# The first MLP matrix's weight sums: built in DRAM scratch by copies and accumulating transfers, or grown in their own SBUF tiles between uses

## The chip, the cores and the metric

The kernel runs on one core of a Trainium2 chip. TensorE multiplies matrices, VectorE, ScalarE and GpSimd (POOL) work elementwise, and transfers are issued on the queues of SyncE (SP), ScalarE (ACT) and POOL and carried out by 16 DMA engines that the queues share. The metric is the device time of one execution in microseconds.

## The reference

Two layers on x of 512 tokens by 1024 features, float32. Each layer has a mixer (a projection of the normalised x into attention, an mLSTM memory and gates, two branch projections, an output projection) and an MLP. The change is in the MLP's weights:

```python
    x = x + mixed @ w_out

    u = jax.nn.relu(rmsnorm(x, norm_ffn) @ w_ff1)
    return x + (u * u) @ w_ff2
```

w_ff1 is 1024 x 4096 and w_ff2 is 4096 x 1024 for each layer.

## The kernel before

**Split products.** Every float32 operand is split into a rounded high part and the rest (ScalarE makes the high part, VectorE subtracts, lines 916 and 917 for the MLP's weights), and a product is three matmuls (`mm3`, line 211). TensorE's work is therefore in matmuls, and ScalarE and VectorE have a split to make for each weight block.

**Seven products instead of eight.** In the MLP, blocks of two by two are multiplied with seven products instead of eight, which needs sums of weight blocks. With b11, b12, b21, b22 the four quarters (row half, column half), the sums are A = b11 + b12, D = b12 + b22, B = b11 + D and C = b21 + B (`SUMS`, line 373). Of the seven products, numbers 1, 2 and 3 use plain quarters (b11, b21, b22) and 5, 6, 7 and 4 use A, B, D and C. The left operands are sums of the other matrix's quarters, made once (`left_blocks`, line 1056, for the first matrix; `left`, line 1013, for the second).

**Parts.** The MLP's width of 4096 is done in four parts of 1024 columns (two times 512). `first(part, i, u)` (line 1096) makes half a part of relu(h @ W1)^2 with seven slots of 24 matmuls 128x256, its accumulators in two PSUM banks of one pair and in two auxiliary banks. `second(part, u)` (line 966) multiplies a part by W2 with seven slots of two runs of 12 matmuls 128x512. Part 0 of the first matrix is done with plain products (`Plain`, line 1153), since its left operand is not ready in time for the sums.

**Order of the work.** Lines 1196 to 1208 write the order out: each slot of `second` is followed by 2, 2, 2, 2, 3, 3 and 0 slots of the next part's two `first` blocks. A unit is one run. `go` (line 1217) prepares the weights of the unit five ahead (`SPL`), that is, it emits its load and its split, and then the unit's matmuls. Five buffers of split weights (`spl`) make a split wait until the matmuls five units back are done. Raw tiles of the first matrix rotate over three buffers (`raws`), loaded on SP's queue by `load1` (line 946); at the head of the MLP the first seven loads are queued behind marked loads of the mixer's output projection (`w_marks`, line 905). Raw tiles of the second matrix (`raw2`) have a buffer of their own by name and half, and many of W2's sums are made in them by VectorE (`plus`, line 924).

**Sums in DRAM.** The sums of W1 for parts 1 to 3, and some of W2 (D of every part, all four of the last part), are built in DRAM scratch (`Sums`, line 385), in halves of 512 KB. Each half of a sum is first copied from the weights (or from another sum) by a transfer on ScalarE's queue, and then a transfer on POOL's queue adds the other addend to it. So that these jobs are spread, each is tied to a split: the copy is queued behind the last split on ScalarE, and the addition behind a marker (line 404), a tiny POOL copy that reads the last split's result. `plan_sums` (line 414) lists the jobs, and `beat` (line 426) does the next one: 32 beats lie in the mixer (line 866), four at the head of the MLP (line 1188), and then one at every second unit (line 1227). A layer has 79 jobs, three of them empty.

Of the kernel before, what the change touches and what calls it, by code (L numbers as in the profile page):

```python
# [8 lines left out]
F32 = mybir.dt.float32  # L9
# [4 lines left out]
ALU = mybir.AluOpType  # L14
# [21 lines left out]
def hybrid_kernel(ctx, tc, x, norm_mix, w_in, att_q_norm, att_k_norm, att_sinks, m_gate_bias,  # L36
# [157 lines left out]
        return wh, wl  # L194

    last_wh = [None, None]
    w_loads, w_marks, by_turns = [], [], []
    last_split = [None, None]

    def split(src, scale=None, get=lambda: slot(F32R)):  # L200
# [66 lines left out]
    def rsqrt(dst, v, tag):  # L267

        shape = list(v.shape)
        t = sm(shape, tag + "t")  # L270
        sc.activation(t, v, AF.Ln)
        sc.activation(dst, t, AF.Exp, scale=-0.5)
        t2 = sm(shape, tag + "u")
# [100 lines left out]
    mark = const.tile([1, 2], F32, name="mark")  # L374
    jobs, sums = [], {}

    def w1_rows(l, part, k, n, h):
        r0, c0 = T * k + 2 * P * h, DFF // 2 * n + T * part
        return w_ff1[l, r0:r0 + 2 * P, c0:c0 + T]
# [5 lines left out]
    class Sums:  # L385
# [11 lines left out]
            return self.to(b, h) if b in SUMS else self.rows(*b, h)  # L397

        def copy(self, n, h):
            with tc.issue_after((last_split if by_turns else last_wh)[0].ins):  # L400
                nc.scalar.dma_start(self.to(n, h), self.of(SUMS[n][0], h))

        def add(self, n, h):
# [9 lines left out]

    def plan_sums(l):

        s = [None] + [Sums(l, part, w1_rows) for part in range(1, 4)]
        p = [Sums(l, part, w2_rows, "D") for part in range(3)] + [Sums(l, 3, w2_rows)]
        sums.clear()
        sums.update({(1, part): s[part] for part in range(1, 4)})
        sums.update({(2, part): p[part] for part in range(4)})  # L420
        jobs.extend(s[1].copies("DABC") + s[1].adds("DAB") + p[0].copies("D") + s[1].adds("C")
                    + s[2].copies("DABC") + p[0].adds("D") + s[2].adds("DAB") + p[1].copies("D") + s[2].adds("C")
                    + s[3].copies("DABC") + p[1].adds("D") + s[3].adds("DAB") + p[2].copies("D") + s[3].adds("C")
                    + p[3].copies("DABC") + p[2].adds("D") + p[3].adds("DAB") + [lambda: None] * 3 + p[3].adds("C"))

    def beat():
        if jobs:
# [2 lines left out]
    def beats(*at):  # L430
        return [(a, beat) for a in at]

    def mixer(l, norm, late, order, phase):
# [134 lines left out]
        def rope(xv, b, nh):  # L568

            r0 = 0 if nh == HQ else 8  # L570
            ct, st = tabs[nh != HQ]
            ve.tensor_tensor(xv, xv, rqk[:, b, r0:r0 + nh].unsqueeze(2).to_broadcast([P, nh, HD]), op=ALU.mult)
            t1 = sm([P, nh, ROPE], f"rp{nh}")
            t2 = sm([P, nh, ROPE], f"rq{nh}")
# [317 lines left out]
    def mlp(l, norm, late, phase):  # L892
# [62 lines left out]
        def gain(t, j, ps, sign, done=False):  # L955

# [9 lines left out]
        def second(part, u):  # L966
# [15 lines left out]
            def weights(which, h):  # L982
                if end:
                    tag = "pqpqpqp"[(1, 5, 6, 3, 7, 2, 4).index(which)]
                    plain = {1: (0, 0), 3: (1, 1), 2: (1, 0)}.get(which)
                    load(b11, tag, h, block(*plain, h) if plain else
                         sums[2, 3].to({5: "A", 6: "B", 7: "D", 4: "C"}[which], h))
                    return w_split(b11[h])
                if which == 1:
                    load(b11, "p", h, block(0, 0, h))  # L990
                    load(b12, "q", h, block(0, 1, h))
                    r = w_split(b11[h])
                    plus(b11[h], b11[h], b12[h])
                elif which == 5:
                    load(b22, "q", h, block(1, 1, h))
                    r = w_split(b11[h])
                    plus(b11[h], b11[h], b22[h])
                elif which == 6:
                    r = w_split(b11[h])
                elif which == 3:  # L1000
                    r = w_split(b22[h])
                elif which == 7:
                    load(b12, "q", h, sums[2, part].to("D", h))
# [92 lines left out]
        def first(part, i, u):  # L1096

            c0 = T * part + H * i
            ps = {}

            def weights(which):
                at = {1: (0, 0), 3: (1, 1), 2: (1, 0)}.get(which)
                if at:
                    k, n = at
                    return load1(w_ff1[l, T * k:T * (k + 1), DFF // 2 * n + c0:DFF // 2 * n + c0 + H])
                return load1(sums[1, part].t[{5: "A", 6: "B", 7: "D", 4: "C"}[which]][:, H * i:H * (i + 1)])

            def to(t, n):
                return u[i][:, 2 * n:2 * n + 2, H * t:H * (t + 1)]
# [13 lines left out]
            def slot(which, bank, fresh, *done):  # L1123

                ws = []

                def run():
                    if fresh:
                        if bank == "a":
                            two = banks("f")  # L1130
                            ps["a"], ps["b"] = two[:, 0, :], two[:, 1, :]
                        elif bank != "b":
# [12 lines left out]

                return Slot([lambda: ws.append(weights(which))], [run], end)

            return [slot(1, "a", True, (copy, 0, 0)), slot(5, "b", True, (copy, 1, 1)),
                    slot(2, "c", True, (finish, 0, 0)), slot(6, "a", False, (copy, 0, 1)),
                    slot(3, "b", False, (finish, 0, 1)), slot(7, "a", False, (finish, 1, 1), (copy, 1, 0)),  # L1150
                    slot(4, "d", True, (finish, 1, 0))]

        class Plain:


            def __init__(self, i, n, which):
                self.c0, self.i, self.n, self.which, self.w = DFF // 2 * n + H * i, i, n, which, {}

            def load(self, h):
                self.w[h] = load1(w_ff1[l, T * h:T * (h + 1), self.c0:self.c0 + H])  # L1160

            def step(self, k):
                if k == 0:
# [19 lines left out]
        for h in range(2):  # L1183
            for f in plain:
                f.load(h)
        by_turns.append(1)
        weave([(0.5, lambda k=k, f=f: f.step(k)) for k in range(KT) for f in plain],
              late + [(6.5, norm.inverse)] + beats(1.6, 2.1, 2.6, 3.1))
        by_turns.clear()
        for f in plain:  # L1190
            f.evac(us[0])
        us.append(new_u(1))
# [24 lines left out]
        def go(i, s, n):  # L1217
# [68 lines left out]
```

## Time and profile before

| | us |
|---|---|
| three runs | 1327.36, 1330.26, 1337.07 |
| median of the runs | 1330.26 |
| the profiled execution's own time | 1333.33 |
| its span, from the first to the last instruction | 1331.5 |
| TensorE busy | 1298.1 |
| VectorE busy | 954.5 |
| ScalarE busy | 768.5 |
| POOL busy | 215.3 |

PE is TensorE, DVE is VectorE, ACT is ScalarE, and a q behind a name is the queue on which it issues transfers. A group's line shows the line of the kernel, the engine, the operation, the tile written and the tile read, the shapes, how often, then the busy time and the mean in ns of one, then the idle time of the engine just ahead of them with what ended it. Tiles are named without their numbers: raw is a raw weight tile, wh and wl its split, sum a sum in DRAM scratch. In the chain of waits a line has a start, a duration and what it was; in a timeline the same, with the idle time ahead of it in brackets. In a table of stretches each engine has its busy time and the number of its instructions, and then come the granted clock, the share of the 16 DMA engines that was busy, and GB/s. In a list of queues q1 is SP's, q10 is ScalarE's and q0 is POOL's, each with packets, MB and their share of the 16 engines' time. In a list of transfers the last number is the median time from issue to landing.

The layers' MLPs lie at about 320 to 650 us and 980 to 1330 us, the mixers ahead of them.

### The profile page before, as it was taken

Reading aid. Unit: us, or ns where it says so; the run is one execution under the profiler, and the core shown is the slowest. Engines: PE = TensorE matmul, PEld = TensorE weight load, DVE = VectorE, ACT = ScalarE, POOL = GpSimd, SP = SyncE. Lnnn points to the kernel's source line nnn. Section 1 sums busy time; section 2 is a strip of 40 time slices with the busy share of each in tenths; the row PEclk is TensorE's granted clock in tenths of the full one; section 3 lists DMA queues with packets and bytes.
Section 4 is the critical chain, followed back from the end, with each engine's and each line's share of the span. In section 5 each row is a group of like instructions: output and inputs, shape, how many; then the busy total and the mean of one; then the engine's idle time right before and its main releaser. Section 6 shows DMA issues by size and latency. Waiting matters only on the chain.

```text
span 1331.5 us, 19392 instructions
## 1 busy us (share of the span) xinstructions
PE 1298.1 (97%) x6966; PEld 1103.2 (83%) x6966; DVE 954.5 (72%) x1493; ACT 768.5 (58%) x1367; POOL 215.3 (16%) x371
## 2 busy tenths in 40 slices
PE   8999999998999999999999999999999999999998
PEld 6877788887888989899778777888888899899986
DVE  4688764475568698887946887644766687979786
ACT  5468765553366556666545687654544565666663
POOL 4523310200000210020005233102000002102100
PEclk9999999999999999999999999999999999999999
DMA  5547455847356989897415465557382579997954
GB/s 151 172 137 148 120 153 150 180 120 216 100 135 230 252 200 285 238 243 223 154 29 181 136 140 127 151 155 170 119 260 71 152 249 242 233 309 198 270 160 142
DMA packets 154176, 236.36 MB, mean 178 GB/s; under 512 B 11608, under 2 KB 67008, under 8 KB 154080
## 3 DMA queue, kind: packets, MB, share of 16 engines
q1 hardware_dynamic: 111776, 154.76, 36.8%
q0 software_dynamic: 21056, 39.98, 18.2%
q10 hardware_dynamic: 21248, 40.38, 9.8%
q8 instruction: 55, 0.90, 0.3%
q14 instruction: 41, 0.34, 0.1%
HBM read 232.99 MB, written 81.79 MB: 236 GB/s over the span
## 4 chain that ended last, share of the span: by engine, by line
PE 78%; DVE 11%; DMA 4%; ACT 3%; issue 3%; POOL 0%; SPq 0%; ACTq 0%; DVEq 0%; POOLq 0%
PE mm L47 67%; PE aux L47 9%; DMA raw<-in_w_ff_dram 3%; PE aux L51 2%; DVE wl L917 2%; DVE wl L193 2%; DMA w<-in_w_in_dram 1%; ACT wh L916 1%; DVE ul L909 1%; DVE x L961 1%; ACT wh L192 0%; DVE s L931 0%; ACT t L658 0%; DVE a L724 0%; DVE t L645 0%
## 5 line engine op out<-in xcount | busy, mean ns | idle before, releaser
L47 PE MATMUL mm<-i,wh 128*128 128x512 f32 (+1 forms) x1280 | 354.4, 362 | 0.5 <-ACT t L842 0.5
L917 DVE TENSOR_TENSOR wl<-raw,wh 128x1024 fp32r<-128x1024 f32 x212 | 257.1, 1220 | 81.2 <-ACT wh L916 81.0
L916 ACT ACTIVATE wh<-raw 128x1024 fp32r<-128x1024 f32 x212 | 223.4, 1055 | 151.4 <-PE mm L47 113.5
L47 PEld LDWEIGHTS mm<-i,wh 128*128 128x128 f32 x1280 | 224.3, 189 | 32.9 <-ACT t L842 0.9
L47 PE MATMUL mm<-i,wl 128*128 128x512 f32 (+1 forms) x640 | 229.7, 359 | 0.0
L193 DVE TENSOR_TENSOR wl<-w,wh 128x512 fp32r<-128x512 f32 (+1 forms) x208 | 142.1, 684 | 110.6 <-ACT wh L192 107.0
L192 ACT ACTIVATE wh<-w 128x512 fp32r<-128x512 f32 (+1 forms) x208 | 126.9, 612 | 135.4 <-PE mm L47 96.6
L404 POOL COPY mark<-wh 1x2 f32<-1x2 f32 x76 | 47.7, 628 | 813.1 <-ACT wh L916 660.1
L47 PE MATMUL mm<-wh,ul 128*128 128x512 f32 x448 | 175.7, 392 | 2.6 <-DVE ul L909 2.1
L47 PE MATMUL mm<-wh,uh 128*128 128x512 f32 x448 | 175.7, 392 | 1.5 <-DVE x L961 1.5
L47 PE MATMUL mm<-wl,uh 128*128 128x512 f32 x448 | 175.2, 391 | 0.6 <-DVE wl L917 0.6
L47 PE MATMUL mm<-wh,i 128*128 128x512 f32 (+1 forms) x512 | 149.7, 370 | 0.4 <-ACT wh L192 0.4
L47 PEld LDWEIGHTS mm<-i,wl 128*128 128x128 f32 x640 | 120.9, 189 | 17.7
L47 PE MATMUL mm<-hs,wh 128*128 128x256 f32 x576 | 105.7, 284 | 0.0
L47 PEld LDWEIGHTS mm<-wh,i 128*128 128x128 f32 x512 | 92.3, 189 | 15.9 <-ACT wh L192 0.8
L47 PEld LDWEIGHTS mm<-wh,ul 128*128 128x128 f32 x448 | 84.4, 188 | 22.4 <-DVE ul L909 5.0
L47 PEld LDWEIGHTS mm<-wh,uh 128*128 128x128 f32 x448 | 84.6, 189 | 18.1 <-ACT wh L916 2.1
L47 PEld LDWEIGHTS mm<-wl,uh 128*128 128x128 f32 x448 | 84.4, 188 | 17.0 <-DVE wl L917 0.9
L47 PE MATMUL mm<-wl,i 128*128 128x512 f32 (+1 forms) x256 | 94.1, 368 | 0.0
L47 PEld LDWEIGHTS mm<-hs,wh 128*128 128x128 f32 x576 | 91.4, 192 | 2.6 <-ACT u L1115 1.0
L961 DVE SCALAR_TENSOR_TENSOR x<-mm,ninv,x 128x512 f32<-128x512 f32 x112 | 80.8, 746 | 16.4 <-PE mm L47 16.4
L47 PE MATMUL mm<-wh,a 128*128 128x512 f32 x256 | 83.3, 399 | 5.2 <-DVE x L885 4.6
(243 smaller groups left out, 2145.8 us busy)
## 6 DMA issues: line engine op xcount, KB each, us to landing
raw<-in_w_ff_dram SPq DMA_DIRECT2D x112, 512.0 KB, 5.7
sum<-in_w_ff_dram ACTq DMA_DIRECT2D x76, 512.0 KB, 4.5
raw<-sum SPq DMA_DIRECT2D x76, 512.0 KB, 5.4
w<-in_w_in_dram SPq DMA_DIRECT2D x128, 256.0 KB, 3.6
sum<-in_w_ff_dram POOLq DMA_DIRECT2D x44, 512.0 KB, 7.5
sum<-sum POOLq DMA_DIRECT2D x32, 512.0 KB, 7.2
w<-in_w_out_dram SPq DMA_DIRECT2D x32, 256.0 KB, 3.3
w<-in_w_att_branch_dram SPq DMA_DIRECT2D x16, 256.0 KB, 3.1
```

Of the source, the lines that this page charges most:

```text
L47: return nc.tensor.matmul(*args, **kw)
L51: return nc.tensor.transpose(*args)
L192: last_wh[:] = sc.activation(wh[:, :off], raw[:, :off], AF.Copy), wh
L193: ve.tensor_tensor(wl[:, :off], raw[:, :off], f32(wh[:, :off]), op=ALU.subtract)
L404: m = gp.tensor_copy(mark, f32(last_wh[1][0:1, 0:2]))
L909: ve.tensor_tensor(lo, src, f32(hi), op=ALU.subtract)
L916: last_wh[:] = sc.activation(hi, r, AF.Copy), hi[:, 0, :]
L917: ve.tensor_tensor(lo, r, f32(hi), op=ALU.subtract)
L961: ve.scalar_tensor_tensor(xh[:, i, :], ps[:, i, :], norm.inv[:, 0 if sign > 0 else 1, b:b + 1], xh[:, i, :], op0=ALU.mult, op1=ALU.add)
```

## The change

The sums of W1 no longer exist in DRAM. For each half part (`first` block) three raw tiles are used, by name: r for the plain b11 (product 1) and b21 (product 2), q for b22 (product 3), and p, of which there are two, so that the next block's can be started. p is loaded with b11 and an accumulating transfer on POOL's queue adds b12 to it, which makes A. After A's split another adds b22 to the same tile, which makes B; after B's split another adds b21, which makes C. In the same way b12 is added to q after b22's split, which makes D. The split reads the tile, so each such transfer waits for the split before it and the next split waits for the transfer. The start of a block (load of p and the first addition) is emitted at product 2 of the block before, and for the first block at the last load of the plain slots.

The products of a block come in the order 5, 1, 3, 6, 2, 7, 4 instead of 1, 5, 2, 6, 3, 7, 4, and the copies and additions out of PSUM are rearranged to suit: product 3's accumulator is copied out and product 6's is added to it.

DRAM scratch is left for W2 alone: 30 jobs a layer, two of them empty, of which 12 are done by the 12 later beats of the mixer and the others at every fourth unit. The other 20 beats of the mixer and the four at the head of the MLP go. To make room for the fourth raw tile, some small scratch tiles (temporaries of `rsqrt` and `rope`) have one buffer instead of three.

The core of the diff:

```diff
-        raws = pool(phase, "raws", 3)
+        raws = pool(phase, "raws", 1)
...
-        def load1(src):
+        def w1_load(tag, k, n, c0):
             with tc.high_priority():
-                r = raws.tile([P, 4, H], F32, tag="raw", name=nm("raw"))
+                r = raws.tile([P, 4, H], F32, tag=tag, bufs=2 if tag == "p" else 1, name=nm("raw"))
                 with ExitStack() as behind:
                     if w_marks:
                         behind.enter_context(tc.issue_after(w_marks.pop(0).ins))
-                    nc.sync.dma_start(r, src.rearrange("(k p) n -> p k n", p=P))
-            return w_split(r)
+                    nc.sync.dma_start(r, w1_block(k, n, c0))
+            return r
+
+        def w1_add(r, k, n, c0):
+            with tc.high_priority():
+                nc.gpsimd.dma_start(r, w1_block(k, n, c0), accum_op=ALU.add)
+
+        def w1_block(k, n, c0):
+            c0 += DFF // 2 * n
+            return w_ff1[l, T * k:T * (k + 1), c0:c0 + H].rearrange("(k p) n -> p k n", p=P)
...
+            def start():
+                load("p", 0, 0)
+                w1_add(r["p"], 0, 1, c0)
+
+            starts.append(start)
+
             def weights(which):
...
+                tag = {1: "r", 2: "r", 3: "q", 7: "q"}.get(which, "p")
+                if which == 1:
+                    load("r", 0, 0)
+                elif which == 3:
+                    load("q", 1, 1)
+                elif which == 2:
+                    load("r", 1, 0)
+                    if starts:
+                        starts.pop(0)()
+                w = w_split(r[tag])
+                more = {5: (1, 1), 6: (1, 0), 3: (0, 1)}.get(which)
+                if more:
+                    w1_add(r[tag], *more, c0)
+                return w
...
-            return [slot(1, "a", True, (copy, 0, 0)), slot(5, "b", True, (copy, 1, 1)),
-                    slot(2, "c", True, (finish, 0, 0)), slot(6, "a", False, (copy, 0, 1)),
-                    slot(3, "b", False, (finish, 0, 1)), slot(7, "a", False, (finish, 1, 1), (copy, 1, 0)),
+            return [slot(5, "b", True, (copy, 1, 1)), slot(1, "a", True, (copy, 0, 0)),
+                    slot(3, "b", False, (copy, 0, 1)), slot(6, "a", False, (finish, 0, 1)),
+                    slot(2, "c", True, (finish, 0, 0)), slot(7, "a", False, (finish, 1, 1), (copy, 1, 0)),
                     slot(4, "d", True, (finish, 1, 0))]
...
-        side += beats(*(2.0 * n for n in range(1, 21)), *(42 + 1.8 * n for n in range(12)))
+        side += beats(*(42 + 1.8 * n for n in range(12)))
...
-              late + [(6.5, norm.inverse)] + beats(1.6, 2.1, 2.6, 3.1))
+              late + [(6.5, norm.inverse)])
...
-            if i % 2:
+            if i % 4 == 1:
                 beat()
```

More of the change, by code (lines that the diff above doesn't have):

```diff
@@ L196, in hybrid_kernel @@
     last_wh = [None, None]
-    w_loads, w_marks, by_turns = [], [], []
+    w_loads, w_marks = [], []
     last_split = [None, None]
@@ L269, in rsqrt @@
         shape = list(v.shape)
-        t = sm(shape, tag + "t")
+        t = sm(shape, tag + "t", 1)
         sc.activation(t, v, AF.Ln)
         sc.activation(dst, t, AF.Exp, scale=-0.5)
-        t2 = sm(shape, tag + "u")
+        t2 = sm(shape, tag + "u", 1)
         ve.tensor_tensor(t2, dst, dst, op=ALU.mult)
@@ L399, in copy @@
         def copy(self, n, h):
-            with tc.issue_after((last_split if by_turns else last_wh)[0].ins):
+            with tc.issue_after(last_wh[0].ins):
                 nc.scalar.dma_start(self.to(n, h), self.of(SUMS[n][0], h))
@@ L414, in plan_sums @@
     def plan_sums(l):
-        s = [None] + [Sums(l, part, w1_rows) for part in range(1, 4)]
         p = [Sums(l, part, w2_rows, "D") for part in range(3)] + [Sums(l, 3, w2_rows)]
         sums.clear()
[L419 to L424, printed above, removed]
+        sums.update({part: p[part] for part in range(4)})
+        for q in p:
+            names = ("D", "DABC")[q is p[3]]
+            jobs.extend(q.copies(names) + q.adds(names.replace("C", "")) + [lambda: None] * 2 * (q is p[3])
+                        + q.adds(names[3:]))
     def beat():
@@ L986, in weights @@
                     load(b11, tag, h, block(*plain, h) if plain else
-                         sums[2, 3].to({5: "A", 6: "B", 7: "D", 4: "C"}[which], h))
+                         sums[3].to({5: "A", 6: "B", 7: "D", 4: "C"}[which], h))
                     return w_split(b11[h])
@@ L1002, in weights @@
                 elif which == 7:
-                    load(b12, "q", h, sums[2, part].to("D", h))
+                    load(b12, "q", h, sums[part].to("D", h))
                     r = w_split(b12[h])
@@ L1099, in first, with load @@
             ps = {}
-            def weights(which):
[L1102 to L1106, printed above, removed]
+            r = {}
+            def load(tag, k, n):
+                r[tag] = w1_load(tag, k, n, c0)
+            def start():
+                load("p", 0, 0)
+                w1_add(r["p"], 0, 1, c0)
+            starts.append(start)
+            def weights(which):
+                tag = {1: "r", 2: "r", 3: "q", 7: "q"}.get(which, "p")
[12 more added lines that the diff above has]
+                return w
             def to(t, n):
@@ L1128, in run @@
                     if fresh:
-                        if bank == "a":
+                        if which == 5:
                             two = banks("f")
                             ps["a"], ps["b"] = two[:, 0, :], two[:, 1, :]
-                        elif bank != "b":
+                        elif bank in "cd":
                             ps[bank] = aux()
@@ L1156, in __init__ @@
             def __init__(self, i, n, which):
-                self.c0, self.i, self.n, self.which, self.w = DFF // 2 * n + H * i, i, n, which, {}
+                self.i, self.n, self.which, self.w = i, n, which, {}
             def load(self, h):
-                self.w[h] = load1(w_ff1[l, T * h:T * (h + 1), self.c0:self.c0 + H])
+                r = w1_load("prpq"[2 * h + self.n], h, self.n, self.i * H)
+                self.w[h] = w_split(r)
+                if self.i + self.n + h == 3:
+                    starts.pop(0)()
             def step(self, k):
```

10 lines of the change are left out of this document (3 added, 7 removed).

## Prediction

> **What bounds the kernel now.** I read the page first, then busy time by stretches, then the chain of waits, then the DMA queues. The page:
>
> ```profile
> span 1331.5 us, 19392 instructions
> PE 1298.1 (97%) x6966; PEld 1103.2 (83%) x6966; DVE 954.5 (72%) x1493; ACT 768.5 (58%) x1367; POOL 215.3 (16%) x371
> ...
> L916 ACT ACTIVATE wh<-raw 128x1024 fp32r<-128x1024 f32 x212 | 223.4, 1055 | 151.4 <-PE mm L47 113.5
> ```
>
> TensorE is idle 1331.5 - 1298.1 = 33.4 us: no relief elsewhere can bring more. The weight sums are used in the MLPs, where a part (28 units, 504 matmuls) takes 79 us. So I asked for slices of 79 us, two of the first layer's MLP and one of the second's:
>
> ```profile
> 434.00:513.00 79.00, 76.88 (x477) 69.27 (x476) 62.59 (x64) 46.24 (x57) 14.54 (x20) 0.98 0.91 232
> 513.00:592.00 79.00, 79.00 (x507) 71.99 (x506) 66.84 (x68) 49.69 (x61) 9.96 (x13) 1.00 0.91 254
> ...
> 1094.00:1173.00 79.00, 79.00 (x507) 71.81 (x506) 66.40 (x68) 49.26 (x60) 13.88 (x20) 1.00 0.97 248
> ```
>
> The first number after the slice's length is TensorE's busy time, the last but one the DMA share. Two slices are full although the engines of the transfers are 0.91 and 0.97 taken. TensorE sets the pace there: a unit is 79 / 28 = 2.82 us. What transfers cost today shows where the layers differ. Both run the same program, and the chain has the same pieces in each:
>
> ```profile
> 264.73 17.71 PE mm L47 x78
> ...
> 309.26 8.29 DMA raw<-in_w_ff_dram
> ...
> 355.33 35.20 PE mm L47 x155
> ...
> 455.94 12.37 DMA raw<-in_w_ff_dram
> ...
> 494.17 19.58 PE mm L47 x120
> ...
> 929.76 17.71 PE mm L47 x78
> ...
> 974.49 4.46 DMA raw<-in_w_ff_dram
> ...
> 1015.20 35.18 PE mm L47 x155
> ...
> 1149.87 19.71 PE mm L47 x120
> ```
>
> From the first pair to the second the layers stand 929.76 - 264.73 = 665.03 and 1015.20 - 355.33 = 659.87 us apart: the first layer lost 5.2 us more, around a load that landed in 8.29 us against 4.46. By the third pair they are 655.70 apart: 4.2 us more, around a load of 12.37 us. These 9.4 us are what late transfers cost. The first place in detail:
>
> ```profile
> 310.46 0.57 POOL L406 DMA_DIRECT2D sum<-sum  x1
> 311.56 0.57 POOL L406 DMA_DIRECT2D sum<-sum  x1
> 317.58 1.06 ACT L916 ACTIVATE wh<-raw 128x1024 fp32r<-128x1024 f32 x1 [6.72 <-DMA raw<-in_w_ff_dram]
> 318.66 1.23 DVE L917 TENSOR_TENSOR wl<-raw,wh 128x1024 fp32r<-128x1024 f32 x1 [7.09 <-ACT wh L916]
> 321.14 0.80 PE L47 MATMUL mm<-wh,a 128*128 128x512 f32 x1 [4.21 <-DVE x L885]
> ```
>
> Two accumulating transfers start 1 to 2 us behind the load; ScalarE waits 6.72 us for the load, VectorE behind it, and the addition to x that frees a bank comes late: TensorE stands 4.21 us and then runs slowly for a few matmuls.
>
> **The change, part by part.** Transfers of 512 KB, over the run:
>
> ```profile
> raw<-in_w_ff_dram SPq DMA_DIRECT2D x112, 512.0 KB, 5.7
> sum<-in_w_ff_dram ACTq DMA_DIRECT2D x76, 512.0 KB, 4.5
> raw<-sum SPq DMA_DIRECT2D x76, 512.0 KB, 5.4
> ...
> sum<-in_w_ff_dram POOLq DMA_DIRECT2D x44, 512.0 KB, 7.5
> sum<-sum POOLq DMA_DIRECT2D x32, 512.0 KB, 7.2
> ```
>
> By the loops, a layer's 6 blocks of the first matrix need 4 plain loads each instead of 3 plain and 4 of sums: loads fall from 188 to 152. Copies in DRAM fall from 76 to 28 (only W2's sums). The accumulating transfers stay 76: 28 in DRAM, 48 new ones into SBUF tiles, in 1 KB pieces instead of 2 KB. What they take of the 16 engines, in the slice 434 to 513 us:
>
> ```profile
> q1 hardware_dynamic: 9349, 11.53, 45.1%
> q0 software_dynamic: 2656, 5.14, 39.5%
> q10 hardware_dynamic: 816, 1.57, 6.4%
> ...
> raw<-in_w_ff_dram SPq DMA_DIRECT2D x13, 512.0 KB, 8.5
> raw<-sum SPq DMA_DIRECT2D x10, 512.0 KB, 5.9
> sum<-in_w_ff_dram POOLq DMA_DIRECT2D x6, 512.0 KB, 8.6
> sum<-in_w_ff_dram ACTq DMA_DIRECT2D x4, 512.0 KB, 5.4
> sum<-sum POOLq DMA_DIRECT2D x4, 512.0 KB, 8.0
> ```
>
> A load: 45.1% of 79 us over 23 = 1.55 us. An accumulation: 39.5% over 10 = 3.12 us. A copy: 6.4% over 4 = 1.26 us. No row shows an accumulation into SBUF. Plain loads cost by the byte, whatever the piece; two slices of the mixer, 30 to 70 us (mean piece 1.31 KB) and 170 to 220 us (1.82 KB):
>
> ```profile
> q1 hardware_dynamic: 3055, 4.01, 34.6%
> ...
> q1 hardware_dynamic: 2016, 3.67, 25.0%
> ```
>
> That is 34.6% x 40 x 16 / 3055 = 72 ns a piece and 99 ns, 55 and 54 ns per KB. So I take 3.12 us for the new accumulation too; the upper bound, the same time per piece with twice the pieces, is 6.24; the lower bound, a plain load, 1.55.
>
> *Engines of the transfers.* A slice after: 18 loads x 1.55 = 27.9 us, 8 accumulations of the first matrix x 3.12 = 25.0. The 18 jobs of the last W2 sums now come every fourth unit (11.3 us): about 5 copies in a layer's first slice, 3 copies and 4 accumulations in the second, 4 accumulations in the third, so 75%, 88% (27.9 + 25.0 + 3.8 + 12.5 = 69.2 of 79) and 83%. The second was 91 and 97%, the third 91. A relief of 3 to 9 points there, no more.
>
> *The added waits.* The accumulation goes into the tile that was just split, so it waits for ScalarE and VectorE and must land before the next split of that tile. Five of a pair of blocks' six such pairs lie 5 units apart in the new order (sums 5 to 6, 3 to 7, and 6 to 4 in the second block), one lies 7 apart: 5 x 2.82 = 14.1 us. Split 1.06 + 1.22 = 2.3 us, then landing 8.6 (8.0 to 8.6 above, after the issue): 10.9, so 3.2 us are left. If it is late, ScalarE stands at that split, and behind it the copies out of PSUM, the squares and the splits of u. But a split is made 5 units ahead of its product (five buffers; ScalarE's row above waits mostly for TensorE, 113.5 us), so TensorE is short only 4 x 2.82 - 2.3 = 9.0 us later still. On POOL's queue each accumulation stands behind the ones before and behind the start of the next block, whose plain load can go out at least 8 units earlier. The loads r and q wait in SP's queue for a split at least 5 units back, as the rotation over three tiles had it before. Cost: 0.
>
> I weigh a rule against this. The new waits matter more if POOL is slow to write its descriptors, and the Trainium skill (SBUF — State Buffer, section "SBUF: two separate sides") says that while VectorE holds the port it shares with GpSimd, a transfer issued from GpSimd is starved of descriptors. By that rule, the accumulations would land later where VectorE is busier. The trace has 8.6 us where VectorE is busy 62.59 of 79 us, and the mixer for comparison:
>
> ```profile
> 225.00:250.00 25.00, 25.00 (x119) 20.89 (x118) 12.23 (x31) 14.64 (x29) 6.44 (x10) 1.00 0.74 155
> ...
> sum<-in_w_ff_dram POOLq DMA_DIRECT2D x6, 512.0 KB, 7.4
> ```
>
> 7.4 us where VectorE is half busy: 1.2 us between the two, and the busier place has more transfers beside it as well: the trace shows little of the rule. The margin of 3.2 us would shrink by no more than that, so the sum stays.
>
> *What leaves the mixer.* 20 of its 32 jobs go: ScalarE's queue saves an issue for each copy, POOL a marker and an issue for each accumulation. Worth nothing, I think: TensorE's waits in the mixers are for VectorE, and the row below stands the same in both layers, whose transfers fell differently:
>
> ```profile
> PE aux L51 <- DVE t L645: 1.7, 3, 1.2
> ```
>
> Without that cover it would be at most the idle time outside the MLPs. The smaller scratch tiles (one buffer for the temporaries of rsqrt and rope) are written and read in order by one engine each: 0. The reordered products (5, 1, 3, 6, 2, 7, 4) have the same matmuls and additions; the left block of product 5 is needed a unit earlier, at about 396 us (two units behind the piece of the chain that ends at 390.5), and is written by 371: 0.
>
> ```profile
> L909 DVE TENSOR_TENSOR hs<-u,hs x3: 1219/1221/1226, 363.7 to 369.7; 128x1024 fp32r<-128x1024 f32 x3
> ```
>
>
> *The sum.* The two accumulations beside the load at 309 us are gone, because no job is left at the head of the MLP: -5.2 us, after which TensorE itself is next, as in the second layer. The stall at 456 us is in the second slice, relieved by 3 points only: I take half, -2.1. From the profiled execution's 1333.33 us (span 1331.5 and 1.8 around it; 3.1 above the median of the runs): 1333.3 - 5.2 - 2.1 = **1326.0 us**. Against the median itself this is -0.3%. Bounds of these terms: both stalls gone, 1323.9; none, 1333.3.
>
> **The rivals.**
>
> *Saturated transfers (slower).* Place: the MLP slices. With the new accumulation at 6.24 us, 8 are 49.9 us of a slice: the slices need 27.9 + 49.9 + 6.3 = 84, 27.9 + 49.9 + 16.3 = 94, and 27.9 + 49.9 + 12.5 = 90 us of 79: 31 us over in a layer, 62 in all, about **1392**. It decides from (79 - 27.9 - 16.3) / 8 = 4.35 us on, so midway between 3.12 and 6.24 (4.68) barely. For it: the accumulations take twice a load's time already. Against: loads cost by the byte.
>
> *Late accumulations (slower).* Up to three stand behind each other on one queue (3, 6 and the next block's start within 4 us). If each landing came after 23 us (14.1 + 9.0) TensorE would starve: at 25 us, 2 us at 10 to 15 places a layer, some 50 us, **1380**. Against: 8.6 us.
>
> *The mixer gains as well.* TensorE is idle 6.2 us in the first slice of 25, which the change can't touch:
>
> ```profile
> 0.00:25.00 25.00, 18.84 (x88) 15.43 (x89) 10.77 (x18) 12.94 (x25) 14.66 (x35) 1.00 0.64 185
> ```
>
> If the copies and markers hold up attention, half of what is idle besides this and the two stalls, (33.4 - 9.4 - 6.2) / 2 = 9 us, goes with the 7.3: **1317**. Against: the equal waits of both layers; for: the jobs' issues stand in ScalarE's and POOL's order.
>
> *It doesn't relieve.* Accumulations now start bound to splits, two or three together, and a load behind them is late as at 309 us: the two stalls stay or move, **1331**.
>
> The Trainium skill (DMA: Bandwidth & Descriptors, section "Anatomy of one DMA — SWDGE (gpsimd) path") gives 2.0 us plus bytes over 436 GB/s for a transfer issued from GpSimd, an estimate of 3.2 us for 512 KB. By that, both slower rivals would be out; the trace has 7.2 to 8.6 us for accumulations, so their chances stay.
>
> **How the numbers follow.** Forecast 0.44; it doesn't relieve 0.17; mixer too 0.15; saturated 0.15; late 0.09. A measurement of this kernel can tell about 1% (13 us) from no change, so the forecast and the third are "same" (0.61), the mixer's case is on the border and I count it faster with 0.15, both slower cases 0.24. The range runs from 1316 to 1350: the low end holds the mixer's case, the high end the beginnings of saturation; the rest of the slower cases lies outside. The likeliest case alone has 1322 to 1333.
>
> **What would show it.** Right: 28 copies and 152 loads; accumulations into raw tiles landing in 7.5 to 10 us; ScalarE's split waits for them together under 20 us; DMA shares of 0.75 to 0.9 in the slices; the load at the head of the first MLP landing in about 4.5 us and no 4.21 us gap behind it; both mixers' spans unchanged within 2 us. Wrong: raw tiles' landings above 14 us, splits waiting for POOL's transfers, slices of 79 us with fewer than 500 matmuls, or a mixer shorter by over 3 us.

## The result, and the profile after

Before 1330.30 us (median of 20 runs, 1324.9 to 1343.42), after 1324.18 us (20 runs, 1321.89 to 1326.63): ratio 0.9943, 95% interval 0.9926 to 0.9961. The forecast was 1326.0 us, "same" within the 1% that it named, range 1316 to 1350. The profiled execution took 1324.14 us, 9.2 less than that of before; the medians differ by 6.1.

From the page after: span, busy times, POOL's DMA queue, its issues of the new accumulations, and the transfers of 512 KB.

```profile
span 1322.4 us, 19224 instructions
...
PE 1296.7 (98%) x6966; PEld 1101.0 (83%) x6966; DVE 953.9 (72%) x1493; ACT 768.4 (58%) x1367; POOL 217.9 (16%) x323
...
q0 software_dynamic: 33344, 39.98, 19.4%
...
L951 POOL DMA_DIRECT2D raw<-in_w_ff_dram x48 | 62.2, 1296 | 522.8 <-DVE wl L911 247.0
...
raw<-in_w_ff_dram SPq DMA_DIRECT2D x124, 512.0 KB, 5.1
raw<-in_w_ff_dram POOLq DMA_DIRECT2D x48, 512.0 KB, 6.5
sum<-in_w_ff_dram ACTq DMA_DIRECT2D x28, 512.0 KB, 5.0
raw<-sum SPq DMA_DIRECT2D x28, 512.0 KB, 4.2
```

The reader is to see that the traffic is the one forecast (124 + 28 = 152 loads, 28 copies, 48 accumulations into raw tiles), and that TensorE's idle time fell from 33.4 us to 1322.4 - 1296.7 = 25.7 us: 7.7 of the 9.1 us by which the spans differ. The other 1.4 are busy time.

Two of the stretches of 79 us that the prediction shows (stretch, then busy time of each engine, granted clock, DMA share, GB/s):

```profile
434.00:513.00 79.00, 79.00 (x504) 71.25 (x503) 66.44 (x68) 48.79 (x59) 17.70 (x16) 1.00 0.92 215
513.00:592.00 79.00, 78.88 (x503) 71.04 (x502) 66.52 (x67) 48.28 (x59) 15.70 (x16) 1.00 0.86 197
```

The first stretch has 504 matmuls instead of 477 although the share of the DMA engines is 0.92 against 0.91: no relief there, and the stall is gone. Its accumulations, and POOL's queue, which carries them:

```profile
q0 software_dynamic: 5120, 5.90, 48.4%
...
raw<-in_w_ff_dram POOLq DMA_DIRECT2D x8, 512.0 KB, 8.0
sum<-in_w_ff_dram POOLq DMA_DIRECT2D x4, 512.0 KB, 7.5
```

The new accumulations by their line: whom they kept waiting, and how long they took to land.

```profile
who waited for it (us, times):
  ACT wh L910: 0.3, 1
...
DMA to landing us min/median/max: 6.0/6.5/12.6
```

Of 48 accumulations a single one kept a split waiting, by 0.3 us. All of ScalarE's waits for raw tiles from w_ff (14.1 us, 15.3 before) are therefore, but for that, waits for plain loads:

```profile
ACT wh L910 <- DMA raw<-in_w_ff_dram: 14.1, 12, 3.5
```

The head of the first MLP, timeline:

```profile
314.44 1.06 ACT L910 ACTIVATE wh<-raw 128x1024 fp32r<-128x1024 f32 x1 [3.50 <-DMA raw<-in_w_ff_dram]
...
318.01 0.50 PE L47 MATMUL mm<-wh,a 128*128 128x512 f32 x1 [0.99 <-DVE x L879]
```

Where the time came from is read best by setting the k-th matmul of one trace against the k-th of the other. Around this place (matmul 1500) after gains 4.6 us. From matmul 2160 to 2400, the place of the load of 12.37 us, it gains 4.7. From 3240 to 3360, the end of the first MLP, it gains 2.5, of which 0.6 are lost again by 3400. The first mixer, up to matmul 1440, is 0.2 us longer, and the second, from 3400 to 4920, 1.6 shorter. In smaller steps elsewhere 4 to 5 us are given back: 8.9 at the last matmul.

The gain at the end of the first MLP has no term in the prediction. Before, one of the last two accumulations of the first layer starts 2.2 us behind a load for the next mixer, and the load takes 6.55 us. Behind it in ScalarE's order stand weight splits, and TensorE waits twice, by 0.6 and 1.5 us:

```profile
624.71 6.55 DMA w<-in_w_in_dram
...
626.94 0.90 POOL L406 DMA_DIRECT2D sum<-sum  x1 [0.24 <-issue]
```

```profile
PE mm L47 <- DVE ul L909: 1.5, 1, 1.5
PE mm L47 <- DVE x L961: 0.6, 1, 0.6
```

After, no accumulation runs there, since the fewer jobs are done earlier, and the load takes 5.14 us; 1.1 us of wait are left at that end:

```profile
617.47 5.14 DMA w<-in_w_in_dram
```

It is the chain of the prediction's first stall in a third place.

### The profile page after: what moved, and what is told of

It is laid out like the page before. It is cut to its first block, busy times and chain, and to the rows that moved or that the text cites. A ratio compares the mean times of both kernels' runs of the same rounds, so it can differ in the third digit from the quotient of the medians.

```text
span 1322.4 us, 19224 instructions
## 1 busy us (share of the span) xinstructions
PE 1296.7 (98%) x6966; PEld 1101.0 (83%) x6966; DVE 953.9 (72%) x1493; ACT 768.4 (58%) x1367; POOL 217.9 (16%) x323
## 3 DMA queue, kind: packets, MB, share of 16 engines
q0 software_dynamic: 33344, 39.98, 19.4%
## 4 chain that ended last, share of the span: by engine, by line
PE 48%; DVE 5%; ACT 2%; DMA 2%; issue 1%; DVEq 0%; POOL 0%; SPq 0%; ACTq 0%; POOLq 0%
PE mm L47 42%; PE aux L47 5%; DMA raw<-in_w_ff_dram 1%; PE aux L51 1%; DVE wl L193 1%; DVE wl L911 1%; ACT wh L910 1%; ACT t L652 0%; ACT wh L192 0%; DMA w<-in_w_in_dram 0%; DVE ul L903 0%; DVE x L965 0%; DVE t L639 0%; DVE t L689 0%; DVE t L616 0%
## 5 line engine op out<-in xcount | busy, mean ns | idle before, releaser
L951 POOL DMA_DIRECT2D raw<-in_w_ff_dram x48 | 62.2, 1296 | 522.8 <-DVE wl L911 247.0
```

The source lines that it names most:

```text
L951: nc.gpsimd.dma_start(r, w1_block(k, n, c0), accum_op=ALU.add)
```

## The experiments

**1. Is the gain the stall at the head?** The kernel before, with the four jobs moved from the head of the MLP into the mixer.

```diff
-        side += beats(*(2.0 * n for n in range(1, 21)), *(42 + 1.8 * n for n in range(12)))
+        side += beats(*(2.0 * n for n in range(1, 21)), *(42 + 1.4 * n for n in range(16)))
...
-              late + [(6.5, norm.inverse)] + beats(1.6, 2.1, 2.6, 3.1))
+              late + [(6.5, norm.inverse)])
```

> The kernel before, with the four jobs at the head of the MLP moved into the mixer's last stretch (16 beats there instead of 12); the sums of the first matrix stay in DRAM. Theory (of the gain, some 5 us are the two accumulations that no longer run beside the load at 309 us): 5 us less than before, about 1325, TensorE's gap behind that load under 1.5 us, the stall at 456 us unchanged. Rival (it is the smaller traffic as a whole): no change, 1330.

Measured: 1328.99 us (12 runs) against 1330.69, ratio 0.9986 [0.9963, 1.0008]: 1.7 us less where 5 were expected, and the interval holds no change as well. Its timeline at the same place:

```profile
314.61 1.06 ACT L916 ACTIVATE wh<-raw 128x1024 fp32r<-128x1024 f32 x1 [2.96 <-DMA raw<-in_w_ff_dram]
...
318.18 0.50 PE L47 MATMUL mm<-wh,a 128*128 128x512 f32 x1 [0.46 <-DVE x L885]
```

The stall at the head is gone in this execution (1327.01 us), and so is the one at 456 us, though no job was moved there. The waits at the end of the first MLP are still there (a load of 7.33 us). Six of its twelve runs took 1326.6 to 1327.7 us and six 1330.3 to 1335.9; those have no trace, so what made the slower six longer is not shown. The second stall seems to depend on more than the order of the work. A stall seen in one profiled execution need not be worth its length in the median.

**2. The reverse:** the changed kernel with two of its jobs at the head of the MLP.

```diff
-        side += beats(*(42 + 1.8 * n for n in range(12)))
+        side += beats(*(42 + 1.8 * n for n in range(10)))
...
-              late + [(6.5, norm.inverse)])
+              late + [(6.5, norm.inverse)] + beats(1.6, 2.1))
```

> The changed kernel, with its last two accumulations of the mixer (W2's D of part 2) moved to the head of the MLP, where the kernel before had two. Theory: the load beside them lands late again and 4 to 5 us come back, about 1329. Rival (traffic as a whole): no change, 1324.

Measured: 1326.61 us, ratio 0.9974 [0.9952, 0.9995], 2.4 us above the changed kernel. Nine runs took 1323.6 to 1327.3 us, three 1332.5 to 1336.0. The profiled execution (1334.75 us) is one of the three:

```profile
311.00 0.57 POOL L402 DMA_DIRECT2D sum<-in_w_ff_dram  x1
...
312.23 0.57 POOL L402 DMA_DIRECT2D sum<-in_w_ff_dram  x1
320.09 1.06 ACT L910 ACTIVATE wh<-raw 128x1024 fp32r<-128x1024 f32 x1 [8.57 <-DMA raw<-in_w_ff_dram]
...
323.66 0.80 PE L47 MATMUL mm<-wh,a 128*128 128x512 f32 x1 [6.06 <-DVE x L879]
```

Two accumulations 1 and 2 us behind the load (at 309.93 us) bring the stall of the prediction's first term back, by its own chain: load, split, addition to x, TensorE. So the mechanism is shown. The load took 10.14 us, and against the changed kernel's trace 7.7 us are lost in this place alone; since nine runs are shorter than this one by 7 us or more, it seems to strike only sometimes.

**3. The mixer's traffic.** The changed kernel with the 20 jobs of the mixer put back; their sums are not used.

```diff
...
+        s = [None] + [Sums(l, part, w1_rows) for part in range(1, 3)]
+        idle_jobs.extend(s[1].copies("DABC") + s[1].adds("DAB") + s[2].copies("D") + s[1].adds("C") + s[2].copies("A"))
...
+        side += [(2.0 * n, lambda: idle_jobs.pop(0)()) for n in range(1, 21)]
```

> The changed kernel, with the 20 jobs that left the mixer (12 copies and 8 accumulations of 512 KB in each layer, with their markers) put back at their old places; their results are not used. Theory (the mixer's time is VectorE's and TensorE's, transfers cost it nothing): within 1.5 us of 1324. Rival (the copies and markers held up attention): 3 to 9 us more.

Measured: 1325.74 us, ratio 0.9952 [0.9931, 0.9973]: 1.6 us above the changed kernel, within the spread of either. The 20 jobs were nearly free, as the prediction had it.

**4. Better than both?** The changed kernel with all of W2's jobs in the mixer.

```diff
-        side += beats(*(42 + 1.8 * n for n in range(12)))
+        side += beats(*(2.0 * n for n in range(1, 21)), *(42 + 1.8 * n for n in range(12)))
```

> The changed kernel, with all of W2's jobs at the 32 beats that the mixer had before, and none in the MLP. Theory (what late transfers still cost in the MLP goes when the slices' DMA shares fall from 0.92 and 0.86 to about 0.7): 1 to 3 us less than 1324, mostly as less spread and no waits of ScalarE for raw tiles. Rival (the remaining waits in the MLP come from the accumulations' own chain): no change.

Measured: 1326.69 us, ratio 0.9963 [0.9948, 0.9979]: 2.5 us above the changed kernel where 1 to 3 less were expected. Against the changed kernel's trace the first mixer loses some 2.6 us up to matmul 480 and the MLPs gain under 1 us each. There was little left to relieve in the MLPs.

**5. More accumulations.** Each accumulation into a raw tile is made twice, so the sums hold their second addend twice.

```diff
-                nc.gpsimd.dma_start(r, w1_block(k, n, c0), accum_op=ALU.add)
+                for _ in range(2):
+                    nc.gpsimd.dma_start(r, w1_block(k, n, c0), accum_op=ALU.add)
```

> The changed kernel, with each accumulation into a raw tile done twice (each sum then has that addend twice). 16 accumulations x 3.1 us take 50 us of a slice, so that the slices need 84, 94 and 90 us of 79. If the engines of the transfers set the pace once they are full: some 60 us more, about 1385. If only lateness counts: landing 2 x 7 us after the split's 2.3 is 16 to 18 us, 2 to 4 late and within the 9 us of margin: no more than 10 us more.

Measured: 1442.75 us, ratio 1.0833 [1.0785, 1.0881], more than either theory gave. First a stretch, then one place in the timeline of ScalarE and TensorE:

```profile
500.00:640.00 140.00, 118.34 (x697) 107.23 (x698) 88.92 (x89) 67.65 (x83) 36.83 (x34) 0.89 0.97 192
```

```profile
499.84 1.06 ACT L910 ACTIVATE wh<-raw 128x1024 fp32r<-128x1024 f32 x1 [11.35 <-DMA raw<-in_w_ff_dram]
500.80 0.58 ACT L1140 ACTIVATE u<-mm 128x512 f32<-128x512 f32 x1
...
501.43 0.58 PE L47 MATMUL mm<-i,wh 128*128 128x256 f32 x1 [12.21 <-ACT u L1140]
```

With the engines of the transfers 0.97 taken, saturation may have a part in this, and the run can't say how much. But the three lines of the timeline show something that the prediction doesn't have. ScalarE waits 11.35 us for a tile. Right behind that split in its order stands a copy out of PSUM (product 5's), and TensorE's next product waits 12.21 us for that copy. The prediction let a split be 9.0 us late before TensorE starves; by that this gap would have been 2.4 us.

**6 and 7. The added waits without their slack.** First the old order of the products with the new sums, then one buffer for p instead of two, with the start of the next block behind product 4's split.

```diff
...
-            return [slot(5, "b", True, (copy, 1, 1)), slot(1, "a", True, (copy, 0, 0)),
-                    slot(3, "b", False, (copy, 0, 1)), slot(6, "a", False, (finish, 0, 1)),
-                    slot(2, "c", True, (finish, 0, 0)), slot(7, "a", False, (finish, 1, 1), (copy, 1, 0)),
+            return [slot(1, "a", True, (copy, 0, 0)), slot(5, "b", True, (copy, 1, 1)),
+                    slot(2, "c", True, (finish, 0, 0)), slot(6, "a", False, (copy, 0, 1)),
+                    slot(3, "b", False, (finish, 0, 1)), slot(7, "a", False, (finish, 1, 1), (copy, 1, 0)),
```

> The changed kernel, with the products in their old order (1, 5, 2, 6, 3, 7, 4): then D's accumulation has one unit (2.8 us) until its split instead of five, and in the second block B's two units. Theory: splits wait some 7 us for it at three places of each pair of blocks; the 9 us between a split and its product cover most of it, and VectorE, 84 percent busy, makes up slowly: 10 to 40 us more. Rival (five buffers ahead cover it all, the order was not needed): no change.

```diff
-                r = raws.tile([P, 4, H], F32, tag=tag, bufs=2 if tag == "p" else 1, name=nm("raw"))
+                r = raws.tile([P, 4, H], F32, tag=tag, bufs=1, name=nm("raw"))
...
-                    if starts:
-                        starts.pop(0)()
...
+                if which == 4 and starts:
+                    starts.pop(0)()
```

> The changed kernel with one p tile instead of two, the next block's load and first accumulation issued behind product 4's split. For the second block of each part, sum A then has one unit until its split, and a load (4.5 us), an issue (1.3 us) and a landing (6.5 us) to go: some 12 us late, 3 beyond the 9 us of margin. Theory: 3 to 6 us more at three places of each layer, 10 to 40 us in all. Rival (the margin covers it): within 3 us of 1324.

Measured: 1427.74 us, ratio 1.0714 [1.0668, 1.076], and 1393.8 us, ratio 1.0468 [1.0425, 1.0511]. The waits of ScalarE, old order:

```profile
ACT wh L910 <- DMA raw<-in_w_ff_dram: 122.3, 27, 9.8
```

The stretch 513 to 592 us, old order:

```profile
513.00:592.00 79.00, 66.63 (x373) 59.78 (x374) 51.31 (x54) 38.75 (x48) 12.11 (x13) 0.87 0.79 179
```

Here the engines of the transfers have room (0.79), so lateness, and not saturation, costs these 100 us: in the old order product 7 follows product 3 directly, and its D has to grow in that product's tile between two units. The reorder that the prediction costed at 0 and the second p tile are what makes the change possible. Both losses are far above the 10 to 40 us expected: what a late split costs was still mis-sized. In the old order the largest of TensorE's waits are not for copies but for additions out of PSUM and for the splits themselves:

```profile
PE mm L47 <- DVE u L1143: 24.4, 12, 3.5
PE aux L47 <- ACT wh L910: 17.0, 6, 3.5
```

So here the split weights ran out as well.

**8. Lateness by itself.** The changed kernel, with the 36 accumulations that follow a split started three units later, behind a marker. No traffic is added.

```diff
...
-                    w1_add(r[tag], *more, c0)
+                    later.append([4, lambda: w1_add(r[tag], *more, c0, True)])
...
+                for e in later:
+                    e[0] -= 1
+                while later and later[0][0] == 0:
+                    later.pop(0)[1]()
```

> Nothing but time is added to the changed kernel: the 36 accumulations that are tied to a split (B, C and D of each block) are started three units after that split, behind a marker that reads the split made then. Worked out: three units of 2.82 us, the split's 1.06, the marker's 1.2 and a landing of 6.5 us make 17.2 of the 14.1 us there are, so each is late by about 3 us, and the traffic is that of the changed kernel. By the prediction's step (TensorE is short only 9.0 us later than a split is late) nothing is lost: 1324 to 1327 us. By the other theory (a late split on ScalarE also holds the copies out of PSUM that stand behind it, and TensorE's next product waits for them; a split can be late only by what is left of one unit, 2.82 - 1.06 = 1.8 us) TensorE loses 1 to 2.5 us at most of them: 1355 to 1410 us, with gaps on TensorE that ScalarE's copies end.

Measured: 1424.11 us, ratio 1.0710 [1.0664, 1.0755]. TensorE's row of the page, whom the accumulations kept waiting, TensorE's waits, and one place in the timeline:

```profile
PE 1332.4 (93%) x6966; PEld 1132.5 (79%) x6966; DVE 956.4 (67%) x1493; ACT 767.6 (54%) x1367; POOL 233.1 (16%) x359
```

```profile
  ACT wh L910: 139.0, 29
```

```profile
PE mm L47 <- ACT u L1143: 75.2, 23, 5.5
```

```profile
461.98 1.06 ACT L910 ACTIVATE wh<-raw 128x1024 fp32r<-128x1024 f32 x1 [6.63 <-DMA raw<-in_w_ff_dram]
462.94 0.58 ACT L1143 ACTIVATE u<-mm 128x512 f32<-128x512 f32 x1
...
463.57 0.80 PE L47 MATMUL mm<-hs,wh 128*128 128x256 f32 x2 [3.42 <-ACT u L1143]
464.17 0.41 PE L47 MATMUL mm<-hs,wl 128*128 128x256 f32 x1
...
468.65 0.41 PE L47 MATMUL mm<-hs,wl 128*128 128x256 f32 x1
```

Splits wait 139.0 us in 29 places, and the copy out of PSUM (line 1143 here) ends 75.2 us of TensorE's waits in 23 places; in the changed kernel it is 2.4 us in 3. A split that ScalarE awaits for 6.63 us, well under 9.0, is a gap of 3.42 us. The span grew by 108.0 us (1430.4 against 1322.4): 72.3 idle and 35.7 busy (1332.4 - 1296.7). Behind this gap the granted clock is 0.50 for some 5 us, and a matmul of 256 columns takes 0.41 us instead of 0.28.

**9 and 10. Copies ahead of splits, an attempt that tried nothing.** In the delayed and in the changed kernel, each unit's weights are prepared behind its matmuls and copies.

```diff
-            prepare(i + SPL)
+            prepare(SPL - 1)
...
                 s.done()
+            prepare(i + SPL)
```

> The delayed accumulations again, and each unit's weights prepared behind the unit's matmuls and copies instead of ahead of them, so that a split is made one unit later and stands behind the copies of that unit. If late splits hurt because they hold the copies out of PSUM, they may now be late by 2.82 us more than before: most of the loss goes, 1324 to 1345 us. If they hurt because TensorE runs out of split weights, the split made a unit later makes it worse: the delayed kernel's time or more.

> The changed kernel without delay, each unit's weights prepared behind the unit's matmuls and copies. By the theory of the held copies the rest of such waits (2.4 us in three places) goes and nothing is lost, since TensorE still has three units of split weights: 1321 to 1325 us. If TensorE needs the splits four units ahead: 1330 us or more.

Measured: 1429.08 us, ratio 1.0739 [1.0699, 1.078], and 1323.13 us, ratio 0.9946 [0.9927, 0.9964]. They say nothing about the theory: the instructions of ScalarE, TensorE, VectorE, SyncE and POOL stand in the order of the kernels without the edit, but for one issue of a transfer that changes places with the split beside it. Splits and copies are both emitted with high priority, which is the likely reason. They count as repeats of experiment 8 and of the changed kernel.

**11. The changed kernel once more.**

> The changed kernel once more, beside the others: 1322 to 1327 us, within 0.2% of the time taken first. If the stalls at the head of the first MLP and at about 456 us depend on chance and not on the two accumulations beside the load alone, they may show in this profile too; if they are gone for good, neither shows.

Measured: 1322.89 us (12 runs, 1321.9 to 1325.2), ratio 0.9939 [0.9919, 0.9959]. Neither stall shows in this profile.

**12. The held copy.** The delayed kernel with the pair of PSUM banks as two tiles. In the delayed kernel a product waits for the copy of the product before it, out of the pair's other bank; here only for that out of its own. The `Relu` of the plain slots that use this pair becomes two, one for each bank.

```diff
+    class Pair:
+        def __init__(self, which):
+            self.t = [psum.tile([P, T], F32, tag=f"{which}{m}", name=nm("mm")) for m in range(2)]
+
+        def __getitem__(self, at):
+            return self.t[at[1]][at[0], at[2]]
...
+        if which == "f":
+            return Pair(which)
         return psum.tile([P, 2, T], F32, tag=which, name=nm("mm"))
...
```

> The delayed kernel (36 accumulations started three units after their split, some 3 us too late) with one thing more: the pair of PSUM banks that a block's products 5, 1, 3, 6 and 7 share is two tiles instead of one. In the delayed kernel each of them waits for the copy of the product before it, though that copy reads the other bank of the pair; now it waits only for the copy out of its own bank, which is two products older. Nothing else in the delay or its traffic changes. If a late split costs time because it holds that copy on ScalarE and the next product waits for it, the tolerance grows from under 2 us to some 8 us and most of the 100 us go: 1324 to 1360 us, and TensorE's waits for ScalarE's copies fall from 75 us to under 25. If the time is lost for the split weights themselves or for the transfers, it stays at 1400 us or more.

Measured: 1375.28 us, ratio 1.0330 [1.0281, 1.0380]. TensorE's waits, ScalarE's waits, and a large gap in the timeline:

```profile
PE mm L47 <- ACT u L1152: 27.0, 10, 9.5
```

```profile
ACT wh L919 <- DMA raw<-in_w_ff_dram: 145.2, 36, 10.2
```

```profile
529.40 1.06 ACT L919 ACTIVATE wh<-raw 128x1024 fp32r<-128x1024 f32 x1 [10.21 <-DMA raw<-in_w_ff_dram]
530.36 0.58 ACT L1152 ACTIVATE u<-mm 128x512 f32<-128x512 f32 x1
...
530.99 0.58 PE L47 MATMUL mm<-hs,wh 128*128 128x256 f32 x1 [9.42 <-ACT u L1152]
```

The splits are as late as in experiment 8 (145.2 us against 149.6), and half of the loss is gone: TensorE waits 27.0 us for copies instead of 75.2. So the held copy is a cause, and about half of the price came from the wait for the other bank. The other half stays, and the expected 1324 to 1360 us was missed, as were the under 25 us of waits: where a split keeps ScalarE waiting 10.21 us, even the copy out of the product's own bank (product 5's, to which product 3 is added) comes too late. The Trainium skill (PSUM — Partial Sum Buffer, section "PSUM bank collisions raise a hardware error") asks that accesses of different engines be kept apart by bank; the pair kept apart as a whole is more than that, and the run shows what it costs once a copy is late. The changed kernel with the pair as two tiles and no delay wasn't run; what is left there of such waits is 2.4 us:

```profile
PE mm L47 <- ACT u L1139: 2.4, 3, 1.0
```

## Why the prediction was right, and where it was not

**The head, -5.2 us: right in that execution, too large for a median.** Measured -4.7 there, and the gap of 4.21 us became 0.99. Experiment 2 brings the stall back and so shows the cause. But before with those four jobs elsewhere is only 1.7 us faster in the median, inside its interval: the term took a stall of one execution as one of every execution.

**The stall at 456 us, -2.1 us: wrong in its reason.** The term gave half the stall to a relief by 3 points of the DMA engines. It went whole (-4.7), and the share in that stretch did not fall (0.91 to 0.92). Experiment 1 lost it too, with the old traffic, and of experiments 1 to 4 none has it: only the one trace of before does. Why it came there is open. What the runs say is that long executions are rarer after the change: none of the 32 runs of the changed kernel in experiment 11 and the result took over 1326.7 us, while most of before's did. What makes them rarer was not isolated.

**The cost of the new accumulation, 3.12 us of the 16 engines: right to about a tenth.** 48.4% of 79 us over 12 is 3.19 us, a mean of eight new ones and four in DRAM; over the whole run a new one comes to 3.48 (worked out in the last section). The upper bound of 6.24, and with it the saturated rival, is out. The shares forecast for the first layer's three slices, 75, 88 and 83%, came as 65, 92 and 86. Landings were faster than the 7.5 to 10 us named, 6.5 us in the median of the run, but 8.0 in the second slice and 12.6 at the longest.

**The added waits, 0: right, by a margin mis-stated.** 14.1 us between splits against 2.3 + 6.5 leaves over 5 us, in the second slice with 8.0 us 3.8, and a split waited once, 0.3 us. The step that failed is the further margin, "TensorE is short only 4 x 2.82 - 2.3 = 9.0 us later still". The prediction named the copies behind a late split and then counted only the split weights. Experiment 8 has TensorE 3.42 us idle behind a split that ScalarE awaited for 6.63: the copy out of PSUM that stands behind the split on ScalarE comes too late for the next product. Experiment 12 bears this out: two tiles for the two banks take half of the loss away. So the late rival decides not from a landing of 23 us but soon after split and landing together pass 14.1 us, and at accumulations late by a few us it costs 100 us, not 50. The forecast held because the first margin was enough.

**The mixer 0, the reorder 0, small scratch 0.** The mixers changed by 0.2 us for the worse and 1.6 for the better, inside the 2 us named; experiment 3 bounds the 20 jobs at about 1.6. That rules out the rival of a mixer that gains 9. The reorder is 0 as it stands, and experiment 6 shows what hides there: without it, 104 us. The small scratch was not tried alone.

**The sum.** -7.3 us was forecast against the profiled execution's 1333.33, and -9.2 came. Against the median -4.3 was forecast and -6.1 came. That the two are this near is in part luck. In the median the head is worth 1.7 to 2.4 us by experiments 1 and 2, not 5.2; the 2.1 at 456 us stand on a stall that one trace alone has; and the 1.9 that are left at the end of the first MLP, which the two traces with the old jobs (before and experiment 1) lose there and those of the changed kernel don't, were left out. No run moves that last pair of accumulations alone, so its share of the 6.1 us is read from traces, not tested. It would fit that the fastest runs differ as well, 1324.9 against 1321.9 us.

## What to carry to other kernels

When a wait is added on an in-order engine, look for the first instruction behind it that another engine needs, not for how far ahead the waiting instruction's own result is made: here that was a PSUM copy with a tolerance of 3 us and less (a wait of 6.63 us became a gap of 3.42, one of 10.21 a gap of 9.42, one of 11.35 a gap of 12.21), while the split itself was given 9. A stall read from one profiled execution may be a chance event until other runs show it; weigh it by how often it comes. And count which tile a dependency is held on: two PSUM banks in one tile made each product wait for the other bank's copy.

## What the runs showed of the hardware

An accumulating transfer of 512 KB into SBUF in 1 KB pieces cost the 16 engines about a tenth more than one in DRAM in 2 KB pieces. Before, all 76 were in DRAM, and POOL's queue took 18.2% of 1331.5 us, 3.19 us for each. After, 19.4% of 1322.4 us are 256.5 us; less 28 x 3.19 for those in DRAM, each of the 48 new ones comes to 3.48 us. Twice the pieces would have made it 6.24: the bytes set most of it. POOL is busy longer with its issue, 1282 ns in the median against 776 ns for one from w_ff into DRAM before; none of TensorE's waits after is put down to POOL. POOL's queue before, and the two rows by line (duration ns min/median/max), before and after:

```profile
q0 software_dynamic: 21056, 39.98, 18.2%
...
L406 POOL DMA_DIRECT2D sum<-in_w_ff_dram x44: 569/776/1017, 96.3 to 1241.5; - x44
...
L951 POOL DMA_DIRECT2D raw<-in_w_ff_dram x48: 1273/1282/1342, 325.7 to 1248.2; - x48
```

In experiment 8 a gap of 3.42 us was followed by about 5 us of slow matmuls (the rows above). Behind a gap of 2.87 us in the same timeline they were at full speed at once:

```profile
450.70 0.50 PE L47 MATMUL mm<-i,wh 128*128 128x256 f32 x2 [2.87 <-ACT u L1143]
...
451.05 0.28 PE L47 MATMUL mm<-i,wl 128*128 128x256 f32 x1
```

The Trainium skill (TensorE: Matmul & The Clock Gate, section "Part 1: The HAM clock gate (the "warmup" mystery)") has the clock gated after an idle window of about 3.4 us, until TensorE has been busy for such a window. The trace agrees with that length: experiment 8 has the clock at 0.50 for 3.4 or 6.8 us at a time (418.2 to 421.6, 462.6 to 469.4). On the gap it doesn't: the two gaps above would fit, but one of 2.65 us was followed by half the clock too:

```profile
416.88 0.50 PE L47 MATMUL mm<-hs,wh 128*128 128x256 f32 x2 [2.65 <-ACT u L1143]
...
418.97 0.41 PE L47 MATMUL mm<-hs,wl 128*128 128x256 f32 x1
```

So a gap of 2.87 us could go by without it, and one of 2.65 us not. About a third of experiment 8's added time, 35.7 of 108.0 us, is busy time that such gaps brought with them.
